# Even mixer of a hybrid decoder trunk rebuilt: attention by pairs of heads with their own projections, column groups at once, whole inverse steps, q projected in the opening

## The chip, the cores and the metric

The kernel runs on one core of a Trainium2 chip. The metric is the device time of one execution in microseconds (us), given as the median of several runs. The profile shows one execution; its engines are PE (TensorE, matmuls), DVE (VectorE), ACT (ScalarE, activations and casts), POOL (GpSimd) and SP (the queue that issues most loads).

## The reference

The program is one inference step of a trunk of two layers for 256 prompt tokens and 8 sample rows, width 1024. Each layer is a half-step FFN, a mixer, and a half-step FFN. The even layer's mixer, cut to what matters here:

```python
proj = h @ w_in_even                       # 26 column blocks of 128: q k v r kr vr wd|ad gd
# 8 stick-breaking heads (64 wide), masked to k_pos < q_pos
z = q @ k.T * scale + bias
w = exp(log_sigmoid(z) + (reverse cumsum of log_sigmoid(-z), shifted))
o_sb = w @ v
# 8 RWKV-7 heads
z_w = w0 + tanh(wd) @ w_w2;  decay = exp(-exp(-softplus(-z_w) - 0.5))
iclr = sigmoid(a0 + ad @ w_a2);  gate = sigmoid(gd) @ w_g2
kk = kr*k_k normalised by rsqrt per head;  kf = kr * (1 + (iclr-1)*k_a)
s = s*w - (s kk)(kk*iclr)^T + v kf^T;  y = s r        # a scan over the tokens
o_rwkv = (groupnorm(y) + bonus) * gate
return concat(o_sb, o_rwkv) @ w_out_even
```

## The kernel before

All activations lie with the width on the partitions and 264 tokens (256 and 8) in the free dimension. A weight chunk of 8 blocks of 128x128 comes by DMA as `raw`, ACT casts it to its high part `wh` (L197) and DVE subtracts to the low part `wl` (L198); `block` then makes three matmuls of 264 columns, wh x high, wh x low, wl x high (L295 to L297). The FFNs before and after the mixer consist of almost nothing else.

The even mixer has four stretches.

The **opening**: six column blocks (`FIRST_IN`: wd|ad, four of kr, gd) are projected from the unnormalised input into tiles `raw` as `new_r` ends. `in_proj` evacuates each one (`fixt`, `pb`), then `rwkv_first` makes tanh of wd, gd and of the two low-rank products `pz` and `pa`, four times each. Behind the last tanh of `ti`, `load_exp_ln` issues by hand a load of the activation table that serves both exp and ln. `rwkv_prep` makes, for each quarter m of the heads, an rsqrt (Ln L803, Exp L804), the decays `E` and `En` (Exp L841, L844) from a scan on DVE, and the operands `ar`, `B`, `K` (`K` on POOL). Meanwhile the r blocks (`NEXT_IN`) are projected.

The **inverse** (`rwkv_inverse`): four `gram` products of B, then six levels. A level multiplies each half S of the heads by 64x64 blocks: `pP`, then `pX`, then `pXT`, each 32 matmuls (16 pairs, whose members sit in different row and column halves of PE), followed by a masked product `ss` on DVE or a copy `st` on ACT. After each half step the driver lets a generator `other_half` run, that projects q, k, vr and v (`pi`).

The **chain** (`rwkv_chain`): four chunks of 64 tokens, each `pW`, `Wn` (ACT), `pU`, `Un` (ACT), `pS`, `S` (DVE), `pY`, then `rwkv_out` (`pgm`, Square, `pgv`, Ln L1058, Exp L1059, ...). Between these stand, from `attention`, the eight heads one after another: scores `z` (four matmuls, two of them on 64 rows of PE; then Identity L1094 and softplus L1138 to L1140: Abs, Exp, Ln), weights `pcs` (Exp L1102), values `pov` into one half of the output partitions, with the v projections ahead; and from `samples`, the sample rows' attention, whose value products `pso` (L1209) are 16 matmuls of 32 output rows by 512 columns, each behind a step of its own, with `vp` loaded by indirect DMA through POOL four ahead.

The **output**: `split_out` casts the attention's result (`xh<-qk`) and the RWKV result (`xh<-YT`), and `po` multiplies by w_out_even; its first half (attention's rows) may run before the last chunk's `pgv`.

The order of instructions on each engine is the scheduler's, from the order of the code, the buffers and `issue_after` hints; ACT table loads other than the one by hand are put in by the compiler ahead of an activation that the table at hand doesn't serve. PSUM tiles come from bank groups (`self.banks`): A for `pi`, B for the RWKV tiles, C for samples, D for attention.

Of the kernel before, what the change touches and what calls it, by code (L numbers as in the profile page):

```python
# [117 lines left out]
def even_order():  # L118
    o = [("w_in_even", 0, k, m) for k in range(KD) for m in FIRST_IN]
    o += [("w_in_even", 0, k, m) for m in NEXT_IN + LAST_IN for k in range(KD)]  # L120
# [98 lines left out]
class Trunk:  # L219
# [383 lines left out]
    def _even(self, ctx, ln_in, ln_out):  # L603
# [42 lines left out]
        ps = [self.ps([128, NO], f"raw{i}", t) for i, t in enumerate(("rk", "rk", "rk", "at", "at", "mm"))]  # L646
# [9 lines left out]
        self.rwkv_first(lora, hv)  # L656
        prep = self.rwkv_prep(hv, bone)
        next(prep)
        self.r_t = self.slot([128, 4, NT], "r_t")
        for mb in NEXT_IN:  # L660
            next(prep, None)
            for _ in self.proj(mb):
                pass
        for _ in prep:
            pass
# [4 lines left out]
        self.vtok = vv[:, 1]  # L670
        self.g2 = g2
# [7 lines left out]
        for i, _ in enumerate(self.rwkv_inverse()):  # L679
            if self.stage < 3:  # L680
                next(side)
            if i < BURST:
                next(side)
            if i >= 4 and i % 3 == 2:
                next(tokens, None)
            if i > 5 and (i % 2 or i > 24):
                next(samples, None)
        while self.stage < 3:
            next(side)
# [3 lines left out]
        for i, _ in enumerate(self.rwkv_chain(bone)):  # L693
            next(gate, None)
            next(side, None)
            next(side, None)
# [26 lines left out]
    def other_half(self, bone, sbb, idb, nmb):  # L723
# [3 lines left out]
        for mb in LAST_IN[:4]:  # L727
            yield from self.proj(mb)
        self.stage = 1
        for mb in LAST_IN[4:12]:  # L730
            yield from self.proj(mb)
            if mb == LAST_IN[7]:
                self.stage = 2
        nc.sync.dma_start(out=a["shift_out"], in_=self.sh_out)
        nc.sync.dma_start(out=a["kv_out"][:, 0], in_=self.k_t)
        self.stage = 3
# [42 lines left out]
    def rwkv_first(self, lora, hv):  # L779
# [3 lines left out]
        wa = self.tmp([128, NT], "wa")  # L783
        nc.scalar.activation(wa[0:64], self.wda[0:64], AF.Tanh)
        nc.vector.tensor_copy(wa[64:128], self.wda[64:128])
        nc.scalar.activation(self.gd, self.gd, AF.Tanh, scale=0.5)
        nc.vector.tensor_scalar(out=self.gd, in0=self.gd, scalar1=0.5, scalar2=0.5, op0=ALU.mult, op1=ALU.add)
        self.lw, self.ti = self.slot([128, 4, NT], "lw"), self.slot([128, 4, NT], "ti")
        for m in range(4):
# [5 lines left out]
            last = nc.scalar.activation(self.ti[:, m, :], pa, AF.Tanh, scale=0.5, bias=hv[:, 4 + m:5 + m])  # L795
# [3 lines left out]
    def rsqrt(self, o, x):  # L799

        nc = self.nc
        with self.tc.issue_after(self.tables.ins):
            nc.scalar.activation(o, x, AF.Ln)  # L803
            nc.scalar.activation(o, o, AF.Exp, scale=-0.5)  # L804
        nc.vector.scalar_tensor_tensor(out=x, in0=x, scalar=-0.5, in1=o, op0=ALU.mult, op1=ALU.mult)
        nc.vector.tensor_tensor(out=x, in0=x, in1=o, op=ALU.mult)
        nc.vector.scalar_tensor_tensor(out=o, in0=x, scalar=1.5, in1=o, op0=ALU.add, op1=ALU.mult)

    def rwkv_prep(self, hv, bone):
# [14 lines left out]
        for m in range(4):  # L824
# [22 lines left out]
            nc.vector.tensor_scalar(out=kki, in0=ti, scalar1=0.5, scalar2=0.5, op0=ALU.mult, op1=ALU.add)  # L847
            nc.vector.tensor_tensor(out=kki, in0=kki, in1=kk, op=ALU.mult)
            kf = ti
            nc.vector.tensor_scalar(out=kf, in0=ti, scalar1=hv[:, 8 + m:9 + m], scalar2=hv[:, 12 + m:13 + m],  # L850
                                    op0=ALU.mult, op1=ALU.add)
# [71 lines left out]
    def rwkv_inverse(self):  # L923
# [18 lines left out]
        for lv in range(6):  # L942
            lm = cst[:, None, C_LVL + 64 * lv:C_LVL + 64 * lv + 64].to_broadcast([128, 8, 64])
            P = {}
            for i, s in enumerate(S):
# [10 lines left out]
                yield  # L956
            if lv == 0:
                continue
            for i, s in enumerate(S):
                if lv < 5:  # L960
# [3 lines left out]
                    yield  # L964
# [3 lines left out]
                yield  # L968
# [108 lines left out]
    def attention(self, sbb, idb, nmb):  # L1077
# [8 lines left out]
        def scores(h):  # L1086
            m, H = h // 2, slice(h % 2 * 64, h % 2 * 64 + 64)
            z = self.ps([128, 384], "z", "at")
            mm(z[:, 0:256], lhsT=self.k_t[H, m, 0:128], rhs=self.q_t[H, m, 0:256], start=True, stop=False)
            mm(z[:, 0:256], lhsT=idb, rhs=nmb, start=False, stop=True)  # L1090
            mm(z[:, 256:384], lhsT=self.k_t[H, m, 128:256], rhs=self.q_t[H, m, 128:256], start=True, stop=False)
            mm(z[:, 256:384], lhsT=idb, rhs=nmb[:, 0:128], start=False, stop=True)
            zb[h], sp[h] = att("zb"), att("sp")
            nc.scalar.activation(zb[h], z, AF.Identity, bias=sbb[:, h:h + 1])  # L1094
            self.softplus(sp[h], zb[h])
# [8 lines left out]
        def values(h):  # L1104
            m, H = h // 2, slice(h % 2 * 64, h % 2 * 64 + 64)
            po = self.ps([128, NP], "pov", "at")
            w = zb[h]
            mm(po[H, :], lhsT=vtok[:, 0, h * 64:h * 64 + 64], rhs=w[:, 0:256], start=True, stop=False)
            mm(po[H, 128:256], lhsT=vtok[:, 1, h * 64:h * 64 + 64], rhs=w[:, 256:384], start=False, stop=True)
            nc.scalar.copy(self.q_t[H, m, :NP], po[H])  # L1110
# [7 lines left out]
        for h in range(10):  # L1118
            m = h // 2
            if h in (0, 2, 4, 6):  # L1120
                yield from self.proj(WV + m)
            if h < 8:
                scores(h)
            if h in (0, 2, 4, 6):
                tokens(m)
            if h == 6:
                nc.sync.dma_start(out=self.a["kv_out"][:, 1], in_=self.v_t)
                self.new_h()
                self.oh, self.ol = self.xh, self.xl
            if 1 <= h < 9:  # L1130
                weights(h - 1)
            if h >= 2:
                values(h - 2)
            yield

    def softplus(self, o, z):
        nc = self.nc
        nc.scalar.activation(o, z, AF.Abs)  # L1138
        nc.scalar.activation(o, o, AF.Exp, scale=-1.0)
        nc.scalar.activation(o, o, AF.Ln, bias=1.0)  # L1140
# [39 lines left out]
    def sample_values(self, idx):  # L1180
# [19 lines left out]
        for e in range(4):  # L1200
            load(e)
        for g in range(2):
            for i in range(8):
                e = 8 * g + i
                if i == 0:
                    po = self.ps([128, 512], "pso", "sa")
                yield
# [3 lines left out]
                if i < 7 and e + 4 < 16:  # L1211
                    load(e + 4)
# [4 lines left out]
            if g == 0:  # L1217
                load(11)
# [719 lines left out]
```

## Time and profile before

| | us |
|---|---|
| median of 3 runs (lowest, highest) | 1181.29 (1178.82, 1181.72) |
| the profiled execution's own time | 1178.93 |
| its span, first to last instruction | 1177.2 |
| PE busy over the span | 1119.5 (95%) |
| DVE, ACT, POOL busy | 886.2, 583.6, 201.9 |
| granted clock of PE, mean | 0.984 |

A share of busy time is a mean over the whole program. The even mixer runs from 216 us to 460 us of the span.

### The profile page before, as it was taken

How to read it: one execution, taken by the hardware profiler on the slowest of the kernel's cores; microseconds unless marked ns; L12 is line 12 of the kernel's file. 1: busy time of each engine (PE TensorE's matmuls, PEld its weight loads, DVE VectorE, ACT ScalarE, POOL GpSimd, SP SyncE). 2: the span in 40 equal slices, each digit the busy share in tenths (PEclk: the TensorE clock that was granted, in tenths of full speed). 3: DMA queues.
4: the chain of work that ended last, by engine and by line, in shares of the span. 5: the costliest groups of instructions: out<-in, count | busy, mean ns of one | idle time of the engine just before them, and what ended most of it. 6: DMA issues, size and time to landing. Idle time of an engine off the chain costs nothing. (4 is left out here: it accounts for less than half of the span.)

```text
span 1177.2 us, 26168 instructions
## 1 busy us (share of the span) xinstructions
PE 1119.5 (95%) x10583; PEld 1062.2 (90%) x10583; DVE 886.2 (75%) x1763; ACT 583.6 (50%) x990; POOL 201.9 (17%) x339
## 2 busy tenths in 40 slices
PE   7999999979999998999999999999958999999996
PEld 7999999978886678999999999999956899999995
DVE  4999755889875859998876797675579689655564
ACT  4544544664245565744454654453461366444442
POOL 0000000354535314111110112000045102000000
PEclk9999999989999999999999999999989999999998
DMA  7654656733564314476775567665573263655551
GB/s 250 229 175 151 210 182 207 209 90 112 163 189 155 118 60 142 144 239 214 274 236 176 156 208 222 203 181 178 162 226 129 89 192 120 203 182 181 188 171 51
DMA packets 66123, 204.95 MB, mean 174 GB/s; under 512 B 13465, under 2 KB 16617, under 8 KB 65745
## 3 DMA queue, kind: packets, MB, share of 16 engines
q1 hardware_dynamic: 56400, 174.09, 47.1%
q0 software_dynamic: 6560, 23.27, 6.2%
q10 hardware_dynamic: 3040, 5.92, 1.6%
q8 instruction: 83, 1.36, 0.5%
q14 instruction: 40, 0.32, 0.1%
HBM read 192.22 MB, written 10.86 MB: 173 GB/s over the span
## 5 line engine op out<-in xcount | busy, mean ns | idle before, releaser
L198 DVE TENSOR_TENSOR wl<-raw,wh 128x1024 fp32r<-128x1024 f32 (+2 forms) x317 | 389.0, 1228 | 182.4 <-ACT wh L197 178.5
L197 ACT CAST wh<-raw 128x1024 fp32r<-128x1024 f32 (+2 forms) x317 | 329.9, 1041 | 348.7 <-issue 108.5
L295 PE MATMUL pd<-hh,wh 128*128 128x264 f32 x704 | 200.8, 285 | 0.0
L297 PE MATMUL pd<-hh,wl 128*128 128x264 f32 x704 | 200.7, 285 | 0.0
L296 PE MATMUL pd<-hl,wh 128*128 128x264 f32 x704 | 199.1, 283 | 0.0
L295 PE MATMUL pg<-xh,wh 128*128 128x264 f32 x648 | 184.5, 285 | 3.0 <-DVE fixc L467 1.8
L297 PE MATMUL pg<-xh,wl 128*128 128x264 f32 x648 | 184.2, 284 | 1.1 <-DVE wl L198 1.1
L296 PE MATMUL pg<-xl,wh 128*128 128x264 f32 x648 | 183.7, 284 | 0.0
L297 PE MATMUL pu<-xh,wl 128*128 128x264 f32 x608 | 172.9, 284 | 1.9 <-DVE wl L198 1.9
L295 PE MATMUL pu<-xh,wh 128*128 128x264 f32 x608 | 172.9, 284 | 0.0
L296 PE MATMUL pu<-xl,wh 128*128 128x264 f32 x608 | 172.7, 284 | 0.0
L295 PEld LDWEIGHTS pd<-hh,wh 128*128 128x128 f32 x704 | 132.4, 188 | 0.6
L297 PEld LDWEIGHTS pd<-hh,wl 128*128 128x128 f32 x704 | 132.6, 188 | 0.2
L296 PEld LDWEIGHTS pd<-hl,wh 128*128 128x128 f32 x704 | 132.4, 188 | 0.0
L295 PEld LDWEIGHTS pg<-xh,wh 128*128 128x128 f32 x648 | 122.4, 189 | 3.6 <-ACT xh L451 2.0
L297 PEld LDWEIGHTS pg<-xh,wl 128*128 128x128 f32 x648 | 121.9, 188 | 1.6 <-DVE wl L198 1.5
L296 PEld LDWEIGHTS pg<-xl,wh 128*128 128x128 f32 x648 | 122.3, 189 | 0.0
L297 PEld LDWEIGHTS pu<-xh,wl 128*128 128x128 f32 x608 | 114.3, 188 | 2.7 <-DVE wl L198 2.7
L296 PEld LDWEIGHTS pu<-xl,wh 128*128 128x128 f32 x608 | 115.0, 189 | 0.0
L295 PEld LDWEIGHTS pu<-xh,wh 128*128 128x128 f32 x608 | 114.9, 189 | 0.0
L295 PE MATMUL raw<-rh,wh 128*128 128x266 f32 x192 | 56.1, 292 | 3.2 <-DVE r L346 2.9
L498 ACT CAST hh<-h 128x264 fp32r<-128x264 f32 x79 | 32.2, 409 | 54.2 <-DVE h L497 54.1
(535 smaller groups left out, 2193.5 us busy)
## 6 DMA issues: line engine op xcount, KB each, us to landing
raw<-in_w SPq DMA_DIRECT2D x308, 512.0 KB, 3.7
raw<-in_w SPq DMA_DIRECT2D x7, 384.0 KB, 4.9
gxd<-gc SPq DMA_DIRECT2D x8, 256.0 KB, 2.7
qb<-qd POOLq DMA_DIRECT2D x8, 256.0 KB, 4.3
FT<-wd POOLq DMA_DIRECT2D x8, 256.0 KB, 5.4
bF<-in_bF POOLq DMA_DIRECT2D x8, 256.0 KB, 4.3
rot<-rotd ACTq DMA_DIRECT2D x5, 384.0 KB, 4.6
rotd<-T POOLq DMA_DIRECT2D x2, 768.0 KB, 5.1
```

The lines of the kernel that those rows point to most:

```text
L197: nc.scalar.copy(wh[:, :w], raw[:, :w])
L198: nc.vector.tensor_tensor(out=wl[:, :w], in0=raw[:, :w], in1=wh[:, :w], op=ALU.subtract)
L295: mm(ps, lhsT=wh, rhs=xh, start=start, stop=False)
L296: mm(ps, lhsT=wh, rhs=xl, start=False, stop=False)
L297: self.last_mm = mm(ps, lhsT=wl, rhs=xh, start=False, stop=stop)
L498: self.last = [nc.scalar.copy(hh[:, m, :], h), self.last_mm]
```

## The change

- Opening: `FIRST_IN` is reordered, and its sixth tile lies in bank group C and no longer in A. Two q blocks (`SOON_IN`) are projected ahead of `rwkv_first`, and the other q blocks alternate with r in `NEXT_IN`.
- Work goes from DVE to ACT: the copy of `wa`, a square in `rsqrt` (one DVE instruction fewer), the +1 on `lw`, the affine of `kki` and of `kf`. The affine of `gd` goes to POOL.
- `rwkv_first` makes gd's tanh last in the code, and the hand-issued table load is put behind that one; `softplus` is now also held behind the table load.
- `rwkv_inverse` yields after both halves of a step and no longer after each.
- `attention` goes by pairs of heads: z's matmuls for two heads stand side by side on the two row halves, `pov`'s on the two column halves. Each pair brings the projections that it needs (`blocks`, from `LAST_IN`), so pair 0 stands in the opening, pair 1 in the inverse, pairs 2 and 3 in the chain.
- `sample_values` loads `vp` in groups of four and issues four `pso` matmuls, one for each 32-column group, at once.

Line numbers of the changed kernel are higher by one up to its rwkv_first, and differ further on.

```diff
-FIRST_IN = [WDA, WKR, WKR + 1, WKR + 2, WKR + 3, WGD]
-NEXT_IN = [WR + i for i in range(4)]
-LAST_IN = list(range(4)) + [WVR + i for i in range(4)] + list(range(4, 12))
+FIRST_IN = [WDA, WGD, WKR, WKR + 1, WKR + 2, WKR + 3]
+SOON_IN = [WQ, WQ + 1]
+NEXT_IN = [WR, WQ + 2, WR + 1, WQ + 3, WR + 2, WR + 3]
+LAST_IN = [WK, WV, WVR, WVR + 1, WK + 1, WV + 1, WVR + 2, WVR + 3, WK + 2, WV + 2, WK + 3, WV + 3]
...
-        ps = [self.ps([128, NO], f"raw{i}", t) for i, t in enumerate(("rk", "rk", "rk", "at", "at", "mm"))]
+        ps = [self.ps([128, NO], f"raw{i}", t) for i, t in enumerate(("rk", "rk", "rk", "at", "at", "sa"))]
...
+        for mb in SOON_IN:
+            for _ in self.proj(mb):
+                pass
+        self.rwkv_first(lora, hv)
...
         wa = self.tmp([128, NT], "wa")
+        nc.scalar.copy(wa[64:128], self.wda[64:128])
         nc.scalar.activation(wa[0:64], self.wda[0:64], AF.Tanh)
-        nc.vector.tensor_copy(wa[64:128], self.wda[64:128])
-        nc.scalar.activation(self.gd, self.gd, AF.Tanh, scale=0.5)
-        nc.vector.tensor_scalar(out=self.gd, in0=self.gd, scalar1=0.5, scalar2=0.5, op0=ALU.mult, op1=ALU.add)
...
-            last = nc.scalar.activation(self.ti[:, m, :], pa, AF.Tanh, scale=0.5, bias=hv[:, 4 + m:5 + m])
+            nc.scalar.activation(self.ti[:, m, :], pa, AF.Tanh, scale=0.5, bias=hv[:, 4 + m:5 + m])
+        last = nc.scalar.activation(self.gd, self.gd, AF.Tanh, scale=0.5)
+        nc.gpsimd.tensor_scalar(out=self.gd, in0=self.gd, scalar1=0.5, scalar2=0.5, op0=ALU.mult, op1=ALU.add)
         with self.tc.issue_after(last.ins):
             self.tables = self.load_exp_ln()
...
+            nc.scalar.activation(s, o, AF.Square)
-        nc.vector.scalar_tensor_tensor(out=x, in0=x, scalar=-0.5, in1=o, op0=ALU.mult, op1=ALU.mult)
-        nc.vector.tensor_tensor(out=x, in0=x, in1=o, op=ALU.mult)
+        nc.vector.scalar_tensor_tensor(out=x, in0=x, scalar=-0.5, in1=s, op0=ALU.mult, op1=ALU.mult)
...
-            nc.vector.tensor_scalar(out=lw, in0=lw, scalar1=1.0, scalar2=None, op0=ALU.add)
+            nc.scalar.activation(lw, lw, AF.Copy, bias=1.0)
...
-            for i in range(8):
-                e = 8 * g + i
-                if i == 0:
-                    po = self.ps([128, 512], "pso", "sa")
-                yield
+            po = self.ps([128, 512], "pso", "sa")
+            for p in range(2):
+                for _ in range(4):
+                    yield
                 with self.tc.issue_after(self.anchor.ins):
-                    mm(po[32 * (i // 2):32 * (i // 2) + 32, :], lhsT=w[:, e * 8:e * 8 + 32], rhs=vp[e],
-                       start=(i % 2 == 0), stop=(i % 2 == 1))
+                    for i, e in enumerate(turns[2 * g + p]):
+                        mm(po[32 * i:32 * i + 32, :], lhsT=w[:, e * 8:e * 8 + 32], rhs=vp[e], start=p == 0, stop=p == 1)
```

ACT, in the opening: the tanhs `lw` and `ti` of the four quarters, then the first quarter's Ln and Exp (`t`), with projection evacuations (`pb`) and weight casts between. Before, and then after:

```order
L795 ACTIVATE ti<-pa,hv 128x264
L792 ACTIVATE lw<-pz,hv 128x264
L795 ACTIVATE ti<-pa,hv 128x264
L776 ACT_TABLE_LOAD
L803 ACTIVATE t_3383<-t_3379 128x264
L590 ACTIVATE pb<-pi 128x264
L804 ACTIVATE t_3383<-t_3383 128x264
L197 CAST wh<-raw 128x1024 x2
```

```order
L785 ACTIVATE ti<-pa,hv 128x264
L768 ACT_TABLE_LOAD
L782 ACT_TABLE_LOAD
L782 ACTIVATE lw<-pz,hv 128x264
...
L198 CAST wh<-raw 128x1024
L796 ACT_TABLE_LOAD
L796 ACTIVATE t_3449<-t_3445 128x264
L591 ACTIVATE pb<-pi 128x264
L797 ACT_TABLE_LOAD
L797 ACTIVATE t_3449<-t_3449 128x264
L830 ACTIVATE lw<-lw 128x264
```

The load by hand (L776, now L768) stood behind the last tanh and now stands between them; the next tanh has a load of its own, and from there Ln and Exp have one each (L796, L797). In the whole program ACT has 13 table loads before and 40 after; from the first tanh of `wa` to the last quarter's `E` they are 2 before and 15 after.

PE, in the chain: one of the sample value products, before (one of 12 such places) and after (one of three places with four).

```order
L295 MATMUL pi<-xh,wh 128x264
L296 MATMUL pi<-xl,wh 128x264
L297 MATMUL pi<-xh,wl 128x264
L1209 MATMUL pso<-vp,sw 32x512
L1020 MATMUL pY<-GK_3987,VT 64x64
```

```order
L1012 MATMUL pY<-ar,S 64x64
L1013 MATMUL pY<-GK_4048,VT 64x64
L1014 MATMUL pY<-GB_3890,Un 64x64
L1223 MATMUL pso<-vp,sw 32x512 x4
L1012 MATMUL pY<-ar,S 64x64
```

The four products of one place go to four different column groups of PE. The last group of four is broken into 2, 1 and 1.

ACT, at the end of the chain: the casts of the attention's result (`xh<-qk`; the one of 8 columns is the samples'), the last chunk's `rwkv_out` (from `pgm`) and the table for sqrt (L385, now L386). Before, and then after:

```order
L1074 CAST xh<-qk 128x4x128 x2
L1074 CAST xh<-qk 128x4x8
L1074 CAST xh<-YT 128x4x64
L1022 COPY YT<-pY 128x4x64
L1281 COPY YT<-psy 128x4x8
L1051 ACTIVATE t_5763<-pgm 128x288
L1058 ACTIVATE t_5764<-pgv,eps 128x288
L1062 ACTIVATE t_5765<-pgv,eps 128x288
L1059 ACTIVATE t_5764<-t_5764 128x288
L385 ACT_TABLE_LOAD
L385 ACTIVATE eps<-eps 128x1
L1063 ACTIVATE t_5763<-t_5764 128x288
```

```order
L1067 CAST xh<-qk 128x4x128 x2
L1044 ACTIVATE t_5755<-pgm 128x288
L1051 ACT_TABLE_LOAD
L1051 ACTIVATE t_5756<-pgv,eps 128x288
L1055 ACTIVATE t_5757<-pgv,eps 128x288
L1052 ACT_TABLE_LOAD
L1052 ACTIVATE t_5756<-t_5756 128x288
L386 ACT_TABLE_LOAD
L386 ACTIVATE eps<-eps 128x1
L1056 ACTIVATE t_5755<-t_5756 128x288
L1067 CAST xh<-qk 128x4x8
L1067 CAST xh<-YT 128x4x72
```

The cast of 8 columns stood four instructions ahead of `pgm`'s square, and now stands behind the three loads of the last `rwkv_out` (L1051 for Ln, L1052 for Exp, L386 for sqrt). On PE the `po` matmuls, which began before the last `pgm`, now all stand behind `pgv`.

## Rows read from the trace of the kernel before

**Rows 1.** Busy time by windows: us, each engine's busy us (instructions), granted clock, DMA.

```profile
216.00:236.00 20.00, 20.00 (x157) 19.59 (x156) 18.77 (x31) 14.98 (x28) 10.21 (x17) 1.00 0.71 209
236.00:291.00 55.00, 47.13 (x359) 42.75 (x357) 47.88 (x99) 32.25 (x68) 29.25 (x69) 0.91 0.33 97
291.00:354.00 63.00, 61.66 (x1177) 55.09 (x1178) 52.31 (x81) 20.48 (x41) 29.54 (x40) 1.00 0.58 174
354.00:434.00 80.00, 79.94 (x756) 51.09 (x757) 53.44 (x96) 45.62 (x107) 28.40 (x36) 1.00 0.37 120
434.00:460.00 26.00, 25.86 (x217) 25.07 (x214) 20.84 (x41) 14.87 (x27) 6.00 (x6) 1.00 0.41 119
```

**Rows 2.** Waits of PE in 216 to 292: total us, times, longest.

```profile
PE pi L295 <- DVE fixt L469: 3.8, 1, 3.8
PE pi L295 <- ACT pb L590: 2.6, 1, 2.6
PE pP L940 <- DVE ss L947: 1.5, 1, 1.5
```

**Rows 3.** The same windows view, behind the two waits of the opening.

```profile
242.30:246.00 3.70, 3.66 (x14) 3.48 (x15) 3.54 (x6) 1.17 (x3) 3.19 (x9) 0.50 0.01 2
...
260.00:266.00 6.00, 4.93 (x28) 4.93 (x29) 5.02 (x11) 1.77 (x5) 5.62 (x16) 0.72 0.23 85
```

**Rows 4.** Timeline of ACT in the opening: start, us, engine, line, [idle before].

```profile
250.97 1.28 ACT L776 ACT_TABLE_LOAD   x1
252.27 0.42 ACT L803 ACTIVATE t<-t 128x264 f32<-128x264 f32 x1
252.60 0.38 ACT L590 ACTIVATE pb<-pi 128x264 f32<-128x264 f32 x1
...
283.68 0.42 ACT L841 ACTIVATE E<-cs 128x256 f32<-128x256 f32 x1 [2.58 <-DVE cs L839]
```

**Rows 5.** Lines of ACT, 216 to 292: busy us, mean ns | idle before.

```profile
L197 ACT CAST wh<-raw 128x1024 fp32r<-128x1024 f32 x17 | 17.8, 1047 | 15.4 <-PE pi L296 9.3 <-PE raw L296 2.4 <-PE pd L296 1.9
...
L803 ACT ACTIVATE t<-t 128x264 f32<-128x264 f32 x4 | 1.7, 424 | 3.0 <-DVE t L832 3.0
...
L841 ACT ACTIVATE E<-cs 128x256 f32<-128x256 f32 x4 | 1.7, 417 | 3.8 <-DVE cs L839 3.8
```

**Rows 6.** Lines of ACT, 292 to 462.

```profile
L1094 ACT ACTIVATE att<-z,sbb 128x384 f32<-128x384 f32 x8 | 4.6, 580 | 5.2 <-PE z L1092 5.2
...
L1138 ACT ACTIVATE att<-att 128x384 f32<-128x384 f32 x8 | 4.2, 523 | 0.1
```

**Rows 7.** Timeline of PE in the inverse's first levels.

```profile
291.46 1.15 PE L940 MATMUL pP<-cst,ss 64*64 64x64 f32 x32 [1.45 <-DVE ss L947]
...
296.31 0.39 PE L295 MATMUL pi<-xh,wh 128*128 128x264 f32 x1
...
297.24 1.15 PE L940 MATMUL pP<-X,ss 64*64 64x64 f32 x32
```

**Rows 8.** Lines of PE, 216 to 460: the sample value products.

```profile
L1209 PE MATMUL pso<-vp,sw 128*32 128x512 f32 x32 | 15.1, 602 | 0.0
```

**Rows 9.** Timeline of PE: one head's z, pcs and pov.

```profile
386.63 0.70 PE L1089 MATMUL z<-qk 64*128 64x256 f32 x2
...
387.96 0.86 PE L1099 MATMUL pcs<-att,cst 128*128 128x384 f32 x2
...
388.97 0.65 PE L1108 MATMUL pov<-att,vv 128*64 128x256 f32 x2
...
389.76 0.27 PE L1003 MATMUL pS<-VT,KT 64*64 64x64 f32 x1
```

**Rows 10.** Timeline of PE in the odd layer: eight matmuls of 32 output columns.

```profile
878.16 0.33 PE L1746 MATMUL z<-zu,sel 128*32 128x72 f32 x8 [0.83 <-ACT zu L1735]
```

**Rows 11.** Timeline of ACT at the end of the chain.

```profile
432.14 1.26 ACT L1074 CAST xh<-qk 128x512 fp32r<-128x512 f32 x3
...
437.04 0.50 ACT L1058 ACTIVATE t<-pgv,eps 128x288 f32<-128x288 f32 x1 [0.84 <-PE pgv L1055]
```

More of the change, by code (lines that the diff above doesn't have):

```diff
@@ L119, in even_order @@
     o = [("w_in_even", 0, k, m) for k in range(KD) for m in FIRST_IN]
-    o += [("w_in_even", 0, k, m) for m in NEXT_IN + LAST_IN for k in range(KD)]
+    o += [("w_in_even", 0, k, m) for m in SOON_IN + NEXT_IN + LAST_IN for k in range(KD)]
     o += [("w_out_even", 0, k, m) for m in range(KD) for k in range(4)]
@@ L670, in _even @@
         self.vtok = vv[:, 1]
+        for mb in SOON_IN:
+            for _ in self.proj(mb):
+                pass
+        self.rwkv_first(lora, hv)
+        prep = self.rwkv_prep(hv, bone)
+        next(prep)
+        self.r_t = self.slot([128, 4, NT], "r_t")
+        for i, mb in enumerate(NEXT_IN):
+            if i < 4:
+                next(prep)
+            for _ in self.proj(mb):
+                pass
+        for _ in prep:
+            pass
         self.g2 = g2
@@ L679, in _even @@
         for i, _ in enumerate(self.rwkv_inverse()):
-            if self.stage < 3:
+            for _ in range(1 + i % 2):
                 next(side)
-            if i < BURST:
-                next(side)
-            if i >= 4 and i % 3 == 2:
+            if i >= 4:
                 next(tokens, None)
-            if i > 5 and (i % 2 or i > 24):
                 next(samples, None)
-        while self.stage < 3:
+        while self.stage < 2:
             next(side)
@@ L694, in _even @@
             next(gate, None)
-            next(side, None)
-            next(side, None)
+            for _ in range(1 + i % 2):
+                next(side, None)
             if i in (0, 4, 7, 10, 13):
@@ L726, in other_half @@
         self.vr_t = self.slot([128, 4, NT], "vr_t")
[L727 to L736, printed above, removed]
         yield from self.attention(sbb, idb, nmb)
@@ L1084, in attention, with scores @@
         att = lambda name: self.tw([128, 384], "att", bufs=6)
[L1086 to L1095, printed above, removed]
+        def scores(m):
+            z = [self.ps([128, 384], "z", "at") for _ in range(2)]
+            for o, k, q, n in ((slice(0, 256), slice(0, 128), slice(0, 256), nmb),
+                               (slice(256, 384), slice(128, 256), slice(128, 256), nmb[:, 0:128])):
+                for i in range(2):
+                    H = slice(64 * i, 64 * i + 64)
+                    mm(z[i][:, o], lhsT=self.k_t[H, m, k], rhs=self.q_t[H, m, q], start=True, stop=False)
+                for i in range(2):
+                    mm(z[i][:, o], lhsT=idb, rhs=n, start=False, stop=True)
+            for i in range(2):
+                h = 2 * m + i
+                zb[h], sp[h] = att("zb"), att("sp")
+                nc.scalar.activation(zb[h], z[i], AF.Identity, bias=sbb[:, h:h + 1])
+            for i in range(2):
+                self.softplus(sp[2 * m + i], zb[2 * m + i])
         def weights(h):
@@ L1102, in weights, with values @@
             nc.scalar.activation(zb[h], zb[h], AF.Exp)
-        def values(h):
-            m, H = h // 2, slice(h % 2 * 64, h % 2 * 64 + 64)
+        def values(m):
             po = self.ps([128, NP], "pov", "at")
[L1107 to L1110, printed above, removed]
+            for w in range(2):
+                for i in range(2):
+                    h = 2 * m + i
+                    mm(po[64 * i:64 * i + 64, 128 * w:256], lhsT=vtok[:, w, h * 64:h * 64 + 64],
+                       rhs=zb[h][:, (0, 256)[w]:(256, 384)[w]], start=w == 0, stop=w == 1)
+            nc.scalar.copy(self.q_t[:, m, :NP], po)
         def tokens(m):
@@ L1116, in tokens, with blocks @@
             nc.scalar.copy(vtok[:, :, m * 128:m * 128 + 128], ps)
[L1118 to L1127, printed above, removed]
+        left = list(LAST_IN)
+        def blocks(n):
+            for _ in range(n):
+                yield from self.proj(left.pop(0))
+        for m in range(4):
+            yield from blocks((2, 2, 2, 0)[m])
+            if m == 0:
+                self.stage = 1
+            scores(m)
+            yield
+            tokens(m)
+            yield from blocks((1, 1, 1, 0)[m])
+            if m == 3:
+                yield
+            for i in range(2):
+                weights(2 * m + i)
+            yield
+            yield from blocks((1, 1, 1, 0)[m])
+            if m == 1:
+                self.stage = 2
+                nc.sync.dma_start(out=self.a["shift_out"], in_=self.sh_out)
+            if m == 2:
+                for i, t in enumerate((self.k_t, self.v_t)):
+                    nc.sync.dma_start(out=self.a["kv_out"][:, i], in_=t)
                 self.new_h()
                 self.oh, self.ol = self.xh, self.xl
[L1130 to L1133, printed above, removed]
+            values(m)
             yield
```

47 lines of the change are left out of this document (21 added, 26 removed).

## The prediction

> **What bounds the kernel now.** The busy shares by windows come first [rows 1]. PE is the bound of the even mixer in all but one stretch: it is busy 61.66 of 63 us in the inverse, 79.94 of 80 in the chain, 25.86 of 26 at the output. The exception is the opening, 236 to 291, where PE is busy 47.13 of 55 us at a clock of 0.91, DVE 47.88 and ACT 32.25. The waits of PE say why [rows 2]: 3.8 us for `fixt` (a PSUM bank that isn't free), 2.6 us for the evacuation `pb`, and 1.5 us at the opening's end for `ss`. Behind each of the first two the granted clock is low, 0.50 and 0.72 [rows 3], that is PE ran at 1.2 instead of 2.4 GHz for a part of these stretches. So the places where time can be won are the opening's waits with their slow stretches, and PE's own work in inverse and chain. The rest of the program (FFNs, odd layer) isn't touched. The sum is made against the profiled execution (1178.93 us, with a span of 1177.2); the median of the runs lies 2.4 us above it.
>
> **The change, part by part.**
>
> *Sample value products.* 32 passes take 15.1 us [rows 8], 0.47 each, one after another. Four at once go to four column groups. That such groups run together is shown by eight matmuls of 32 columns within 0.33 us, where 72 columns are streamed [rows 10]. I take 8 passes of 0.47 to 0.55 and about 1.2 for the last group, which is broken in three: 5.3 us, a gain of 9.8. The bounds are 0 (they run in turn) and 11.3 (8 x 0.47).
>
> *Scores and values by pairs.* One head's z takes 386.63 to 387.96, 1.33 us; its pov 388.97 to 389.76, 0.79 [rows 9]. Four passes of z (two of 256 columns, two of 128) are on 64 rows, roughly 1.05 us of the 1.33; side by side a pair saves 0 to 1.05, four pairs 0 to 4.2. No row shows row halves with all columns in use side by side; the nearest are the inverse's 64x64 pairs, 32 matmuls in 1.08 us [rows 7], which do overlap, so I take 3. For pov the column groups of [rows 10] are nearer: half of 1.58 per pair, 3 in all.
>
> *Whole inverse steps.* A half step is followed by six `pi` in 0.93 us (296.31 to 297.24, [rows 7]), where back-to-back `pi` take 0.12 each, 0.72: 0.2 per switch. With the switches halved, some 15 to 20 fewer, I take 3.5. Below nothing is possible if a whole step leaves too little between it and the next, which needs its DVE result; the 9 us in which DVE is idle in this stretch [rows 1] speak against more than 1 or 2.
>
> Together PE has some 19 us less to do, and 11 more could come from the opening's waits and slow clock (6.4 in the two waits, and 0.09 of 55 us, 5, by the clock [rows 1]).
>
> *ACT in the opening.* Here the trace and the new order must be read together. ACT had 32.25 us of work in the window [rows 1]. Added are: 13 table loads of 1.28 [rows 4] = 16.7; four instructions per quarter that came from DVE, and the copy of `wa`, at 0.42 [rows 5] = 7; pair 0's two Identities (0.58) and six softplus steps (0.52) [rows 6] = 4.3; one more weight cast (1.05, [rows 5]) with two evacuations = 1.8. That is 62 us, less 0.09 where one instruction starts before the last ends (252.60 against 252.69, [rows 4]), about 72 times: 55.5 us. From 236.5 ACT would be busy without a gap until 292; with some 3 us of waits that can't be filled, the last `E` starts at 295, where it started at 283.68 [rows 4]. From there to the first pP (291.46, [rows 7]) it was 7.8 us, of which I keep 6: first pP at 301, 9.5 us later. DVE's relief (about 6 us in this stretch) changes nothing, since ACT is now the later of the two.
>
> In return PE has by then done what came later before: 24 more `pi` (2.9), pair 0's z and pcs (4.7), the grams of K (1.9), 9.8 us with a transpose. So the opening ends level: the waits won are spent on table loads.
>
> By the Trainium skill (ScalarE: Activation LUTs, sections Table sets: the hidden batching unit and What ACT_TABLE_LOAD costs) ln and exp share one set and should cost one load, which is what the kernel had by its hand-issued load; the page gives 1.28 us for the load and 1.38 more for a drain at every switch. The trace agrees with the load (1283 ns) and shows no drain: Ln starts 1.30 us after the load did [rows 4]. By the page's full price the 13 loads would add another 18 us to the opening.
>
> *Inverse.* It loses 30 `pi` (3.6), grams (1.9) and switches (3), and takes in pair 1 (5 to 6): 60 to 61 us instead of 63. DVE is busy 52 of 63 there and gains some 5 of pair 1's work, so it is nearly full but not over. pW then starts at about 362 (354 before).
>
> *Chain.* From its start at about 354 [rows 1] to the end of the last pgv at 437, where Ln starts [rows 11], it is some 82.5 us now. Off it come 9.8 (pso), 6.3 (z: two pairs remain, faster), 4 (pcs), 4 (pov), 0.7 (transposes); six `pi` more add 0.7: 58.4. Now ACT's loads count: `Wn`, `Un` and `YT` are copies on ACT on which PE waits, and in a chain that is a third shorter less work lies between. A load of 1.28 ahead of Wn in three chunks, of the sample rows' weights and of pair 3's weights I put at 6.7 us. The last pgv ends at 362 + 65 = 427.
>
> *End.* Before, the last `xh<-qk` cast was done by 433.4, long before Ln at 437.04 [rows 11], and po filled the wait for `rwkv_out`. Now that cast stands behind Square, Ln, Exp and three loads: 3 x 1.28 + 4 x 0.4 = 5.5 us in which PE has no po. po then starts at 432.5 to 433.5, runs 24 us (26 in the last window, with pgm and pgv) and ends at 457. A gap of this size was followed by a slow clock twice [rows 3]; that costs 1.7 to 3.4: 459 to 460.
>
> **Sum:** the output ended at 460 before and ends at about 460 after: the 19 us of PE's work and the 11 of the opening are lost again to ACT's lateness. As unmodelled waits lie on one side I add 1.5: +0 to +3, of a profiled time of 1178.9 about 1180.5, and on the median's level **1183 us**.
>
> **The rivals.**
>
> *Loads hidden (faster).* In the chain ACT has 34 us free of 80 [rows 1]; if the loads fall into waits that ACT has anyway, the 6.7 us vanish, and if the order at the end lets the cast through earlier, the 5.5 and 2.5 do. Then 15 us come off: about 1168 on the median's level. For it speaks ACT's share of the chain; against it that each load stands directly ahead of an instruction that is late itself. It decides where PE's waits between 362 and the first po total less than 3 us.
>
> *ACT and DVE take turns in the opening (slower).* My 3 us of waits assume that ACT always has other work. But before, ACT stood idle 3.0 us for Ln's and 3.8 us for E's operand [rows 5] with half the work; each quarter goes ACT, PE, DVE, ACT, DVE. If these 6.8 stay on top of a full ACT, and each chunk's Wn waits for 2 us more, it is 7 + 5 = 12 us more: 1195. It decides where the first pP comes after 305.
>
> *A load costs twice its length (slower).* If ACT had to empty before each load, up to another 1.28 us would go with each; 13 in the opening are 17 us: over 1199. [Rows 4] speak against it: the instruction behind the load starts 1.30 us after it. I give it 0.03. The drain that the Trainium skill names (ScalarE: Activation LUTs, What ACT_TABLE_LOAD costs) would be this.
>
> *Pairs and groups run in turn.* If z and pov gain nothing, 6 us come back on PE, part of it under ACT's waits: 1187. The change would then not do what it does by its form.
>
> *Loads without effect on the path at all*, opening included: the first pP at 291, 460 - 25: 1158.
>
> **How the numbers follow.** No change can be told from a difference of under 0.3% (1177.8 to 1184.8), about what the runs scatter. The forecast (1177 to 1190) has 0.50, of which 0.27 falls within 0.3%, 0.20 above and 0.03 below it. Hidden loads have 0.21, loads without effect 0.03, turns in the opening 0.19, loads of twice the length 0.03, no concurrency 0.04. Faster is 0.27, the same 0.27, slower 0.46. The range of 8 in 10 goes from the faster rival, 1167, to the slower, 1197; the forecast's own is 1177 to 1190.
>
> **What would show it.** In the profile after: 40 table loads of 1.28 on ACT, 15 of them before the first pP; ACT without idle time from 237 on, PE with some 12 us of waits in the opening; the first pP at 301 (below 296, the opening is won; above 305, the slower rival holds). pso in 5 us and z of a pair in 1.6 to 2.0. PE's waits on Wn, Un and pcs of 6 to 7 us; at the end 5 us before the first po with a slow clock behind them. The prediction is wrong if the loads' places on ACT turn out to have slack, or if the inverse, with PE's steps halved in number, waits for DVE.

## The result, and the profile after

The changed kernel takes 1191.41 us (median of 4 runs, 1189.96 to 1195.76) against 1180.05 before (4 runs, 1178.47 to 1181.72): a ratio of 1.0103, 95% interval 1.0076 to 1.013. It is slower, by about 11 us. That lies in the stated range (1167 to 1197), on the side that had 0.46. It is 8 us above the time that was forecast, and 1.4 us outside the forecast's own range (1177 to 1190). The profiled execution took 1189.96 us with a span of 1187.8, which is 10.6 more than the span before. The last po of the mixer ends at 470.5 where it ended at 459.9, which is the same 10.6 us: the rest of the program is unchanged.

By windows, with the columns of [rows 1] and the bounds set at the first pP, the first pW, the end of the last pgv, the first po and the end of the last po:

```profile
236.00:306.50 70.50, 55.94 (x417) 47.85 (x415) 48.35 (x88) 60.48 (x111) 28.77 (x70) 0.93 0.32 97
306.50:369.50 63.00, 59.27 (x1178) 52.75 (x1176) 53.66 (x87) 26.62 (x52) 27.94 (x40) 1.00 0.47 142
369.50:440.30 70.80, 62.96 (x713) 42.93 (x712) 45.55 (x81) 47.25 (x94) 29.39 (x36) 0.95 0.45 145
440.30:445.00 4.70, 0.30 (x1) 0.14 (x1) 2.64 (x9) 4.58 (x9) 0.79 (x1) 0.96 0.01 3
445.00:470.50 25.50, 25.47 (x194) 25.09 (x194) 19.44 (x34) 11.06 (x17) 4.14 (x4) 0.94 0.34 105
```

The opening ends 15.1 us later than before (306.6 against 291.5); the inverse takes 63.0 as it did; from pW to the last pgv it is 70.7 us instead of 82.5; and from there to the last po 30.2 instead of 22.9. ACT is busy 60.48 of 70.5 us in the opening, where it was busy 32.25 of 55, and 4.58 of 4.7 in the gap before po.

The waits of PE, first from 216 to 320 us:

```profile
PE pn L823 <- ACT t L821: 5.0, 3, 2.7
PE pcs L1097 <- DVE att L1154: 3.7, 1, 3.7
PE pi L296 <- ACT qk L586: 1.7, 2, 1.3
PE pP L932 <- DVE ss L939: 1.7, 1, 1.7
```

and from 320 to 480:

```profile
PE pU L989 <- ACT Wn L985: 3.4, 3, 2.1
PE pso L1223 <- DMA vp<-in_cache_v,idx: 3.0, 3, 2.0
PE po L296 <- ACT xh L1067: 2.9, 1, 2.9
...
PE pst L1236 <- DVE soc L1233: 1.5, 1, 1.5
```

The two waits of [rows 2], for `fixt` and `pb`, are gone but for 0.9 us. In their place stand others, 14.6 us up to the first pP where there were 8.3. Of the 16.6 us up to 320, 8.9 are for ACT; the 3.7 for `att` are for the last step of a softplus, for which DVE itself had waited 3.2 us for ACT. The timeline of ACT ahead of the last quarter's `E` shows the form that this takes:

```profile
284.95 1.03 ACT L1091 ACTIVATE att<-z,sbb 128x384 f32<-128x384 f32 x2
286.00 1.28 ACT L796 ACT_TABLE_LOAD   x1
287.30 0.42 ACT L796 ACTIVATE t<-t 128x264 f32<-128x264 f32 x1
287.63 0.51 ACT L1151 ACTIVATE att<-att 128x384 f32<-128x384 f32 x1
288.15 1.28 ACT L797 ACT_TABLE_LOAD   x1
289.45 0.42 ACT L797 ACTIVATE t<-t 128x264 f32<-128x264 f32 x1
...
290.62 1.28 ACT L1153 ACT_TABLE_LOAD   x1
...
293.12 1.28 ACT L1152 ACT_TABLE_LOAD   x1
...
295.42 1.28 ACT L1153 ACT_TABLE_LOAD   x1
...
297.57 1.28 ACT L834 ACT_TABLE_LOAD   x1
298.87 0.42 ACT L834 ACTIVATE E<-cs 128x256 f32<-128x256 f32 x1
```

Six loads stand in 14 us, four of them because pair 0's softplus (L1151 to L1153) has been taken between the last quarter's Ln and its `E`. Loads don't overlap with their neighbours: one starts 0.02 us behind the end of the instruction ahead (285.98, 286.00) and is followed 0.02 us behind its own end, where two activations overlap by 0.09.

The timeline of ACT at the end of the chain, beside [rows 11]:

```profile
438.64 0.40 ACT L1044 ACTIVATE t<-pgm 128x288 f32<-128x288 f32 x1
439.06 1.28 ACT L1051 ACT_TABLE_LOAD   x1
...
441.26 1.28 ACT L1052 ACT_TABLE_LOAD   x1
...
443.01 1.28 ACT L386 ACT_TABLE_LOAD   x1
...
444.75 0.20 ACT L1067 CAST xh<-qk 128x32 fp32r<-128x32 f32 x1
```

The cast of 0.20 us that lets po begin waits behind three loads, and the first po starts at 445.01. Last, the sample value products on PE (other work stands between the rows, and the third place of four, at 427.2, isn't among them):

```profile
387.35 1.07 PE L1223 MATMUL pso<-vp,sw 128*32 128x512 f32 x8
...
396.73 1.05 PE L1223 MATMUL pso<-vp,sw 128*32 128x512 f32 x4
399.79 2.54 PE L1223 MATMUL pso<-vp,sw 128*32 128x512 f32 x4 [2.00 <-DMA vp<-in_cache_v,idx]
```

```profile
432.15 1.04 PE L1223 MATMUL pso<-vp,sw 128*32 128x512 f32 x2 [0.23 <-DMA vp<-in_cache_v,idx]
433.97 1.04 PE L1223 MATMUL pso<-vp,sw 128*32 128x512 f32 x2 [0.78 <-DMA vp<-in_cache_v,idx]
...
435.74 1.04 PE L1223 MATMUL pso<-vp,sw 128*32 128x512 f32 x2
...
438.55 1.04 PE L1223 MATMUL pso<-vp,sw 128*32 128x512 f32 x2
```

Four column groups at once do eight passes in 1.07 us; one group alone takes 1.04 for its two. But the second place of four waits 2.0 us for `vp` between its second and third product, and the last four run one by one.

### The profile page after: what moved, and what is told of

Its sections match the earlier page's. It is cut to its first block, busy times and chain, and to the rows that moved or that the text cites. A ratio compares the mean times of both kernels' runs of the same rounds, so it can differ in the third digit from the quotient of the medians.

```text
span 1187.8 us, 26178 instructions
## 1 busy us (share of the span) xinstructions
PE 1111.3 (94%) x10583; PEld 1059.2 (89%) x10583; DVE 880.4 (74%) x1745; ACT 620.4 (52%) x1030; POOL 201.2 (17%) x340
## 5 line engine op out<-in xcount | busy, mean ns | idle before, releaser
L499 ACT CAST hh<-h 128x264 fp32r<-128x264 f32 x79 | 32.2, 409 | 56.4 <-DVE h L498 56.3
```

The lines of the kernel that those rows point to most:

```text
L499: self.last = [nc.scalar.copy(hh[:, m, :], h), self.last_mm]
```

## The experiments

All are compared with the kernel before, run on the same chip. Differences between experiments are those of their ratios, times 1180 us. Each ratio is known to within 1.5 to 3.5 us, so a difference of less than some 4 us between two experiments can't be told from none. Times of stages and places are those of one profiled run each.

**The load behind the last tanh again.** Only the place of the hand-issued load is undone.

```diff
-            nc.scalar.activation(self.ti[:, m, :], pa, AF.Tanh, scale=0.5, bias=hv[:, 4 + m:5 + m])
-        last = nc.scalar.activation(self.gd, self.gd, AF.Tanh, scale=0.5)
+            last = nc.scalar.activation(self.ti[:, m, :], pa, AF.Tanh, scale=0.5, bias=hv[:, 4 + m:5 + m])
+        nc.scalar.activation(self.gd, self.gd, AF.Tanh, scale=0.5)
```

> The changed kernel with one thing undone: the table load that serves exp and ln is issued behind the last tanh of ti again, so that the built program has 13 table loads and not 40. Theory (the extra loads eat the savings): 13 loads fewer ahead of the first pP, which comes at 288 to 291 us in place of 306.6; PE's waits for Wn, pcs and the last xh cast (10 us in the changed kernel) go below 3; the mixer's last po ends at 438 to 444 in place of 470.5 (459.9 in the kernel before): 1160 to 1166 us, ratio to the kernel before 0.982 to 0.988. Rival (ACT and DVE taking turns in the opening, with DVE work moved to ACT, is what delays it, loads or not): the first pP stays above 298, the time comes down by 10 us at most, to about that of the kernel before.

It took 1168.65 us, ratio 0.9893 (0.9872 to 0.9914): 25 us below the changed kernel by the ratios, and faster than the kernel before. The first pP is at 289.0, the last po ends at 448.2. The rival falls; the theory's time was 3 to 9 us too good. Its stages by windows (columns of [rows 1], bounds as in the table of the changed kernel) and the waits of PE that remain:

```profile
236.00:289.00 53.00, 47.61 (x378) 42.67 (x377) 44.89 (x85) 41.77 (x95) 26.87 (x68) 1.00 0.38 119
289.00:355.50 66.50, 62.19 (x1215) 55.04 (x1214) 54.78 (x89) 25.61 (x54) 31.01 (x42) 1.00 0.50 142
355.50:419.20 63.70, 60.69 (x713) 41.45 (x712) 45.12 (x81) 32.92 (x82) 32.38 (x36) 1.00 0.51 161
419.20:422.50 3.30, 0.34 (x2) 0.14 (x1) 2.69 (x9) 3.15 (x7) 1.20 (x1) 1.00 0.03 5
422.50:448.20 25.70, 25.70 (x194) 25.32 (x194) 19.42 (x36) 10.95 (x17) 4.89 (x4) 0.93 0.37 111
```

```profile
PE pso L1223 <- DMA vp<-in_cache_v,idx: 2.5, 3, 1.8
PE pn L823 <- ACT t L821: 2.0, 2, 1.2
...
PE po L296 <- ACT xh L1067: 1.5, 1, 1.5
```

In the opening ACT is no longer the later engine, and Wn and pcs are not in the list. Against the changed kernel the opening is 17.5 us shorter, the chain 7.0 and the end (from the last pgv to the last po) 1.2; the inverse is 3.5 longer.

Two places were too good in the theory. The inverse takes 66.5 us from pP to pW. PE has 2.8 us more to do there than in the changed kernel, 1.9 of it for `gram` matmuls of K: all 64 stand here, where the changed kernel had 32 of them done in its longer opening. And the end takes 29.0 us, where it took 22.9 in the kernel before. Of the three loads only sqrt's is left there, yet the gap between the last pgv and the first po is still 3.3 us. The sample rows' result is late (PE waits 1.5 us for `soc`), and its cast stands behind the last `rwkv_out`, as in the changed kernel.

**The defect alone, in the kernel before.** The load goes behind gd's tanh, which stays where it was.

```diff
-        nc.scalar.activation(self.gd, self.gd, AF.Tanh, scale=0.5)
+        last = nc.scalar.activation(self.gd, self.gd, AF.Tanh, scale=0.5)
...
-            last = nc.scalar.activation(self.ti[:, m, :], pa, AF.Tanh, scale=0.5, bias=hv[:, 4 + m:5 + m])
+            nc.scalar.activation(self.ti[:, m, :], pa, AF.Tanh, scale=0.5, bias=hv[:, 4 + m:5 + m])
```

> The kernel before with the one defect alone: the load that serves exp and ln is issued behind gd's tanh, which comes ahead of the tanhs of lw and ti; 46 table loads in the built program, no other edit. Theory (a load costs its 1.28 us wherever its instruction is waited for): first pP later by 6 to 10 us, the chain longer by 5 to 10, po held at the end by 3 to 5: 14 to 24 us slower than the kernel before, ratio 1.012 to 1.020. Rival (ACT is half idle in these stretches, so that loads hide): less than 5 us slower, ratio below 1.004.

1197.08 us, ratio 1.0133 (1.0112 to 1.0154). In the profiled run, the slowest of the five (1199.88), the first pP is at 298.5 (+7.0) and the last po ends at 479.5 (+19.6). Two of its waits of PE, and its chain by windows:

```profile
PE pn L830 <- ACT t L828: 4.4, 2, 3.5
...
PE z L1089 <- ACT qk L1110: 2.1, 1, 2.1
```

```profile
361.50:456.60 95.10, 89.29 (x778) 55.83 (x778) 55.43 (x101) 75.17 (x131) 29.93 (x36) 0.93 0.33 101
```

That is 15.7 us slower, within the theory's 14 to 24; the rival falls. The stages share it otherwise than the theory had it. The chain is 12.6 us longer where 5 to 10 were expected: 5.8 us are waits of PE, and the rest goes with the granted clock, 0.93 where it was 1.00 [rows 1]. And po isn't held at the end: it starts at 454.2, ahead of the last pgv, and from pgv to the last po it takes 22.8 us, as before. 33 loads (42 us of ACT) cost 16 us here, and 27 cost 25 in the new order.

**Eight loads more.** The order stays that of the first experiment, and loads of the same table are put ahead of the Exp of `rsqrt` and behind it.

```diff
-            nc.scalar.activation(o, x, AF.Ln)
-            nc.scalar.activation(o, o, AF.Exp, scale=-0.5)
+            ln = nc.scalar.activation(o, x, AF.Ln)
+        with self.tc.issue_after(ln.ins):
+            self.load_exp_ln()
+            ex = nc.scalar.activation(o, o, AF.Exp, scale=-0.5)
+        with self.tc.issue_after(ex.ins):
+            self.load_exp_ln()
             nc.scalar.activation(s, o, AF.Square)
```

> The kernel of e1_load_last with two more table loads per quarter in the opening, of the table that is loaded anyway: ahead of the Exp of rsqrt and behind it, 8 in all, at the places of most of the extra ones in the changed kernel; the order on ACT is otherwise as in e1_load_last (in the changed kernel pair 0's softplus also stood ahead of the last E). Theory (a load is paid whole at these places: 1.28 us and the overlap with its neighbours, some 1.4): ACT had 15 us idle in the opening of e1_load_last, so a part is covered; the first pP 5 to 10 us later than 289, the time 5 to 10 us over e1_load_last. Rival (it was not the loads' length but the order that came with them, pair 0's softplus ahead of the last E): less than 3 us.

Ratio 0.9974 (0.9961 to 0.9988), 9.6 us over the first experiment's; first pP at 298.3, 9.3 later. The last `E` is only 5.2 later (287.64 against 282.44); the rest is PE's work, delayed by ACT's evacuations, which hold the bank of the next `pi`, and run at a granted clock of 0.95 up to the first pP where it was 1.00:

```profile
PE pi L296 <- ACT pb L591: 5.2, 3, 2.0
```

The theory holds, at the upper end: by the time, a load at such a place costs some 1.2 us though ACT has idle time elsewhere. In the profiled run part of it comes back behind the first pP: the last po ends 6.7 later. Up to the first pP, 8 loads make 9.3 of the 17.5 us by which the changed kernel's first pP is later than the first experiment's. The other 5 extra loads and pair 0's softplus ahead of the last `E` share the rest; they weren't taken apart.

**Heads in turn.** The order of z's and pov's matmuls, in the kernel of the first experiment.

```diff
                     mm(z[i][:, o], lhsT=self.k_t[H, m, k], rhs=self.q_t[H, m, q], start=True, stop=False)
-                for i in range(2):
                     mm(z[i][:, o], lhsT=idb, rhs=n, start=False, stop=True)
...
-            for w in range(2):
-                for i in range(2):
+            for i in range(2):
+                for w in range(2):
```

> The kernel of e1_load_last with z and pov in the order of one head after the other (the same matmuls, the same places, no two row or column halves side by side). Theory (side by side saves 1.05 us per pair in z and 0.75 in pov, and PE is the bound in inverse and chain): 4 to 7 us slower than e1_load_last. Rival (PE waits for something else where pairs stand, so it is worth nothing): within 1.5 us of e1_load_last.

Ratio 0.9934 (0.9908 to 0.9959), 4.8 us more than the first experiment, inside the theory's 4 to 7, with intervals that overlap slightly. The trace shows that only half of the edit reached PE. For z it did: two heads one after the other cost PE 11.2 us in all where pairs cost 7.3, so row halves do run side by side. For pov it didn't: the scheduler put the two heads' matmuls next to each other again, and pov costs 3.4 us against 3.7. So the time bears on z alone; that pov gains by its column halves is read from the traces (6.4 us before, 3.6 in the changed kernel) and wasn't tested by itself.

**Sample value products in turn.** `sample_values` of the kernel before, in the kernel of the first experiment.

> The kernel of e1_load_last with the sample value products of the kernel before: 16 places, one column group each, vp loaded four ahead. The changed kernel's trace has four at once in 0.95 us for 8 passes, but its last group is broken and takes 3.9, and PE waits 3.0 us for vp. Theory (half of the expected gain is lost there): 3 to 6 us slower than e1_load_last. Rival one (the loss is whole, by waits for vp): within 1.5 us. Rival two (the whole gain of 9.8 shows once the loads are gone): 9 us or more slower.

Ratio 0.9943 (0.9922 to 0.9964), 5.9 more: by its size the theory's half gain. In the profiled run only 2.4 us of it are in the chain, where pso costs PE 14.5 us instead of 9.7 but waits 2.1 us less for `vp`. Another 2.7 are at the end: the attention's last cast comes later, and PE waits 4.5 us for it ahead of po, where it waited 1.5.

**Half steps.** The yields of the inverse, with the projections' pieces spread over the halves by the caller.

```diff
                     nc.scalar.copy(P[i], ps)
-            yield
+                yield i
```

> The kernel of e1_load_last with the inverse yielding after each half step, as before: where a whole step is followed by two pieces of projection, one of them now stands between its halves; the rest as in e1_load_last. Counted from the traces, the steps and projections of the inverse cost 30.2 us and 0.140 per pi where they stand whole, 32.1 and 0.152 where they stand in halves, 3.3 us together. About half of the steps are split here. Theory (switching costs PE, and PE is the bound in the inverse): 1 to 3 us slower than e1_load_last. Rival (with whole steps PE waits for DVE's results instead, so that halves are as good or better): within 1 us, or faster.

Ratio 0.9927 (0.9899 to 0.9955); the interval overlaps that of the first experiment, and the last po of the profiled run ends at 447.8, as there. In the inverse alone the theory shows: 68.3 us from pP to pW against 66.5. In the time it isn't decided.

**Two column groups at once.** In `sample_values` of the first experiment, eight places with two products each, `vp` loaded two places ahead.

```diff
-        turns = [[8 * g + 2 * i + p for i in range(4)] for g in range(2) for p in range(2)]
+        turns = [[8 * g + 4 * q + p, 8 * g + 4 * q + 2 + p] for g in range(2) for q in range(2) for p in range(2)]
```

> The kernel of e1_load_last with the sample value products in eight places of two column groups and vp loaded two places ahead (four buffers in use all the time), in place of four places of four. Two at once should take 0.95 us for 4 passes, 7.6 in all, where e1_load_last has 9.7 with 2.5 of waits for vp and 3 of waits at the end (pst, the last xh cast). Theory (the groups of four are spoilt by the buffers: five pages, so the next four loads can't start before the last four products are done): 3 to 7 us faster than e1_load_last, ratio to the kernel before 0.983 to 0.987. Rival (the waits only move to another late result, the last pov and its cast): within 1.5 us of e1_load_last.

Ratio 0.9902 (0.9874 to 0.993), no different from the first experiment. The products take 8.0 us, their waits for `vp` are gone from the list, and the last pgv ends at 414.5 instead of 419.2, as the theory has it. But another wait grows, from 1.5 us, as the rival has it:

```profile
PE po L296 <- ACT xh L1067: 4.5, 1, 4.5
```

**Two groups, and attention faster.**

```diff
-            for _ in range(1 + i % 2):
+            for _ in range(2):
                 next(side, None)
```

> The kernel of e6_column_pairs with attention advanced by two steps for each step of the chain, in place of one and two in turn. There the last pgv ended at 414.5, 4.7 us earlier than in e1_load_last, but the cast of the attention's result stood behind the last rwkv_out and PE waited 4.5 us for it. Theory (that wait is all that hides the gain): the cast stands ahead of the last Ln again, po fills the wait, its start is at 411 to 415 and its end at 437 to 441: 5 to 9 us faster than e1_load_last, ratio to the kernel before 0.981 to 0.986. Rival (attention taken earlier makes PE wait for its ACT results within the chain): within 2 us of e6_column_pairs.

1165.15 us, ratio 0.9877 (0.9859 to 0.9895): the lowest of all, 1.2% ahead of the kernel before and 2.2% of the changed one (against the first experiment its interval overlaps). The wait for `xh` is gone from the list, po starts at 422.4 and ends at 446.8 in the profiled run. The theory's 5 to 9 us are not there: 3 us against the kernel with two groups, and the intervals overlap. The wait was removed, but the last pgv moved from 414.5 to 422.8. Of that, 3.6 us are pso, whose pairs run in step in fewer places (11.6 us against 8.0), and 2.2 are more waits of PE in the chain.

**q later, and bank A again.**

```diff
-        ps = [self.ps([128, NO], f"raw{i}", t) for i, t in enumerate(("rk", "rk", "rk", "at", "at", "sa"))]
+        ps = [self.ps([128, NO], f"raw{i}", t) for i, t in enumerate(("rk", "rk", "rk", "at", "at", "mm"))]
...
-        for mb in SOON_IN:
-            for _ in self.proj(mb):
-                pass
         self.rwkv_first(lora, hv)
         prep = self.rwkv_prep(hv, bone)
         next(prep)
+        for mb in SOON_IN:
+            for _ in self.proj(mb):
+                pass
```

> The kernel of e1_load_last with the opening's order undone in part: the sixth raw tile in bank group A again, and the two first q blocks behind rwkv_first and the first step of prep in the code. Theory (3.8 us of wait for a bank and the slow clock behind it are what the new opening removes): the wait for fixt is back and the first pP comes 3 to 6 us later: 3 to 6 us slower than e1_load_last. Rival (in the opening DVE and ACT set the end, and PE's wait is cover): within 1.5 us.

Ratio 0.9949 (0.993 to 0.9969), 6.6 more; first pP at 292.6. That is slightly over the theory in time, and within it at the first pP (3.6 later). The named wait is not there: none for `fixt` is in its list. The last `E` even comes 2.0 us earlier (280.5); but PE waits 8.2 us ahead of the first pP where it waited 5.4, 2.2 of them ahead of the first `pz` and 2.4 for an attention evacuation, and the granted clock is 0.97 up to there, where it was 1.00.

**DVE keeps its work.** The moves from DVE to ACT and POOL undone, in the kernel of the first experiment.

```diff
-            nc.scalar.activation(lw, lw, AF.Copy, bias=1.0)
+            nc.vector.tensor_scalar(out=lw, in0=lw, scalar1=1.0, scalar2=None, op0=ALU.add)
```

> The kernel of e1_load_last with the work that the change moves from DVE to ACT (and gd's affine to POOL) back on DVE. In e1_load_last DVE is busy 49.9 of 58 us in the opening and ACT 43.3; 17 instructions back make it about 56 and 36. Theory (DVE is then the later one in the opening): first pP 2 to 5 us later, 2 to 5 us slower. Rival (the chain of quarters, not an engine's sum, sets the end; the moves only change where a step waits): within 1.5 us, or faster.

Ratio 0.9954 (0.9938 to 0.997), 7.2 more, with the first pP at 295.7, 6.7 later: somewhat over the theory. But the theory's reason isn't there: from 236 to 289 DVE is no fuller than in the first experiment (44.2 us against 44.9). The timelines show another. First the copy of `wa` on ACT in the first experiment, then the same copy on DVE here, and the first `pz` on PE, which reads `wa`:

```profile
238.45 0.41 ACT L776 COPY wa<-wda 64x264 f32<-64x264 f32 x1 [1.15 <-DVE wda L602]
```

```profile
249.23 0.29 DVE L776 COPY wa<-wda 64x264 f32<-64x264 f32 x1
```

```profile
249.73 0.68 PE L781 MATMUL pz<-wa,lora 128*128 128x264 f32 x2 [3.00 <-POOL E L806]
```

On DVE the copy stands behind other work, 10.8 us later, and the first `pz` comes at 249.73 instead of 243.23. (The view puts PE's wait down to POOL; the copy ends later, at 249.53.) So the place of one small copy gives a delay of the size seen, 6.5 us. It wasn't moved alone, so what the other moves cost stays open.

## Why the prediction was right in sign, and 8 us short

**What bounds, and the loads.** The reading held: the gain of the opening and of PE's savings is there (13 us faster than before without the extra loads) and the 27 loads take it back and more. Their price, with the order on ACT that came with them, is shown by undoing them: 25 us. But the prediction set a gain of 30 us (19 of PE's work, 11 of the opening) against them and had 1158 for loads without effect; without the extra loads it is 1168.65. In that kernel the chain is 18.8 us shorter than before and the opening 2.4, but the inverse is 3.5 longer and the end 6.1. So gain and loss were both put too high, and in part the two errors cancel.

**Opening, forecast +9.5, measured +15.1: with the chain the step that was mis-sized most.** ACT's work came out right, 56.3 us busy up to the last `E` (forecast 55.5), but by luck in part. The 32.25 us it starts from hold 4.4 that stand behind the last `E`, and the overlap is taken off a busy time that is already free of it, some 4 us too much. The waits that can't be filled were 6.1 us and not 3, so that `E` started at 298.87 (forecast 295); and from there to pP it took 7.7 us, as before, where I had kept 6. The part of the slower rival that was to be decided at 305 came true (306.6). Of its mechanism, turns between ACT and DVE, the trace has 2.9 us (ACT's waits for `cs`, E's operand) and nothing for Ln's operand, where the rival had 6.8; the loads are the cause, as the first experiment shows.

**Inverse, forecast 60 to 61, measured 63.0.** PE was busy 59.3 us, about as thought; the waits, all for DVE (1.7 for `ss`, 0.4 for `X`, 0.9 and 0.7 at its end for `bon`), came on top. An inverse that waits for DVE was one of the signs that the prediction named against itself.

**Chain, forecast 65, measured 70.7.** The term of pso failed: 9.7 us and not 5.3, counted from each start to the next. The concurrency is as argued, about 1.0 us for four groups' eight passes, but I let only the last four be broken and at 1.2 us. They cost 3.9; the second four cost 3.5, of which 2.5 for the two products behind the wait, out of step and at a slow clock; and 3.0 us of waits for `vp` stand beside them. The five buffers of `page`, which the prediction never counted, set when the next four loads may start: with `vp` loaded two places ahead these waits are gone (two column groups at once). z and pov by pairs save 3.5 and 2.7 (forecast 3 and 3), whole steps 3.3 (3.5), counted the same way; of these only z was tested in the time, at 4.8 with an uncertainty almost as large. PE's waits for ACT in the chain are 3.4 (Wn), with 0.9 for the sample rows' softplus, where I had 6.7, but behind them and behind those for `vp` the clock is low (0.95 over the chain, where it was 1.00 before).

**End, forecast 5.5 and a slow clock.** Between the last pgv and the first po there are 4.7 us, with two of the three loads in them (the first ends with that pgv), and the granted clock was 0.78 from 445 to 452. This step was right in size. The loads are only a part of it: with two of the three gone, in the first experiment, 3.3 us of the gap stay, because the sample rows' cast stands behind the last `rwkv_out` in either kernel.

**The other rivals.** Loads hidden falls by the first experiment, and z's pairs in turn by that with heads in turn. Loads of twice the length: the load is 1.28 us in all rows, and the instructions ahead of it and behind it stand 0.02 us away. The Trainium skill (ScalarE: Activation LUTs, Table sets: the hidden batching unit) has one load for ln and exp together. The times agree with its worth: the kernels in which the two share a load are 16 and 25 us faster than their like. But it isn't had by itself: in the changed kernel Ln (L796) and Exp (L797) have a load each.

## What to carry to other kernels

Where an activation table is loaded by hand, tie the load to the last activation that needs the table before, and look for the loads in the built order: one activation behind it undoes it for the rest of the program, and no diff shows that. A group of products that runs at once needs its operands at once: count the buffers, since a group as large as the pool can't be loaded ahead. And when an engine's work is only shortened, look which late cast or load the next stage waits for; 4.7 us won in the chain were not to be found in the time. The same holds at the head of a stage: a copy of 0.3 us, moved to another engine, stood behind other work there and put off the first `pz` by 6.5 us.

## What was not expected of the hardware

PE's granted clock can fall behind a short wait. In the changed kernel the wait of 2.0 us for `vp` at 397.8 is followed by a stretch at 0.76. The four passes ahead of the wait take 1.05 us, the four behind it 2.54, in part because their two products are out of step, in part by the clock: the first of them lasts 0.65 us and the other three 1.05 to 1.06 each. Not every such wait does it: behind the 1.8 us for `vp` in the first experiment's kernel the clock stayed at 1.00. The view by windows of the changed kernel, behind that wait and behind the one for po:

```profile
399.00:406.00 7.00, 6.21 (x44) 3.14 (x45) 3.04 (x6) 1.56 (x4) 3.86 (x5) 0.76 0.71 227
...
445.00:452.00 7.00, 6.99 (x47) 7.00 (x48) 3.93 (x9) 1.48 (x2) 0.00 (x0) 0.78 0.00 0
```

Two matmuls on 64 rows each, with all 128 output columns, start 7 ns apart and run side by side. Pair 0's z, 12 passes, takes 1.60 us up to the next instruction, where one head's six took 1.33 [rows 9]:

```profile
279.45 0.70 PE L1085 MATMUL z<-qk 64*128 64x256 f32 x4 [0.22 <-ACT qk L586]
...
281.05 0.39 PE L1161 MATMUL pq<-cst,qk 128*8 128x128 f32 x2
```
